# Fixing TensorE's order in a mixture-of-experts stage, and transposing two experts' rows at once

## The chip, the cores and the metric

The kernel runs on one core of a Trainium2 chip. The metric is the device time of one execution in microseconds (us). The core has five engines with queues of their own: TensorE (PE in the profile; PEld is its weight load), VectorE (DVE), ScalarE (ACT), GpSimd (POOL) and SyncE (SP), which here issues most of the DMA transfers.

## The reference

Two layers of a transformer over 512 latent and 256 context tokens of width 1024, float32. Each layer has four mixers (convolution, gating, neighbourhood attention, latent attention) and then a mixture of 32 experts, of which each token takes two. The change touches only the mixture:

```
def hier_moe(h, w_grp, b_grp, w_exp, b_exp, w_gate, w_up, w_down):
    # routing: the best of 4 groups, in it the best 2 of 8 experts, with weights
    ...
    # for every expert e, over the rows routed to it:
    #   y = (silu(rows @ w_gate[e]) * (rows @ w_up[e])) @ w_down[e]      1024 -> 512 -> 1024
    # result of a token: the weighted sum over its two experts
x = x + g2 * f
```

Layer 0 does this for 768 tokens, layer 1 for the 512 latent ones. The weights of one expert are 6 MB (w_gate and w_up 1024 x 512, w_down 512 x 1024, float32), 201 MB a layer.

## The kernel before, in words

Experts are taken in an order with fixed row capacities. In layer 0 they are 96, 96, 32, 32, 128, 32, 128, ..., and the last twelve 64, 96, 64, 96, 64, 64, 96, 64, 96, 96, 64, 64; in layer 1 96, 96, 32, 32, 32, 96, 32, 96, ..., 96, 96, 32, 32, 32, 32. An expert is named here by its place in this order.

**Weights.** SyncE's queue streams them from HBM into 34 slots of 512 KB (tiles named `u`, `xa`, `xb`, `xc`, hi and lo; eight transfers at most are under way). gate and up of an expert are 8 slots, down is 4. `load()` issues as far as slots are free; a slot comes free when TensorE has done its last matmul with it. The weights of experts 0 and 1 and part of 2's are in place before routing is done; those of expert 3 wait for gate_up(0)'s slots, later ones for gate_up(1)'s and down(1)'s.

**Rows.** `gather(g)` fetches the rows of a group of experts from DRAM with an indirect DMA on GpSimd (L1728) into one of three buffers `xb`. A group is one expert, or two neighbours of at most 64 rows each, which then stand at partitions 0 and 64. `rows(e)` (L1381) turns an expert's rows into columns with eight transposes into PSUM (`xTw`), which VectorE copies to `XT` (L1383), one set of eight per expert.

**Products.** `products` (L1414) does the matmuls of `gate_up(e)` and `down(e)`. Rows beyond 64 make a second part: 96 rows are a part of 64 (each matmul with 512 columns of the result) and one of 32 (256 columns). Within a part neighbouring matmuls go to different columns of the array (`tile_position`). ScalarE does the silu (L1429) and VectorE the product (L1430); `hT(e)` (L1449) transposes these inner values for `down(e)`. ScalarE (layer 0, L1472) or VectorE (layer 1, L1474) copies down's result out, and GpSimd scatters it to DRAM (L1775).

**Order.** The loop runs over `seq`: gu0, gu1, d0, gu2, d1, ..., gu31, d30, d31, with hT(e-1) and rows(e+1) written behind gate_up(e). A scheduler builds each engine's list of instructions; it may move transposes and products of independent tiles past each other.

**The tail.** The last two experts of layer 0 (four of layer 1) are not scattered. `tail_table` builds, over the last third of the loop, a matrix that places their rows (`tail_place`, L1350, L1352); `tail_scale` (L1366) spreads the gate weights over a [128, 1024] tile (ScalarE copy L1368), by which `tail_rows` (L1483, VectorE) multiplies the tail experts' results as they come. After the loop, for each of the six (four) tiles of 128 tokens, `accumulate` adds what was scattered and reloaded (`yload`, L1817: ScalarE scales one of the token's two rows, L1492, VectorE does L1495 to L1497), a product `tailw` (L1804) adds the tail (L1805), and `finish` begins the next norm (L1824 to L1831).

## Time and profile before

| | |
|---|---|
| median of 3 runs | 1890.05 us (1889.16 to 1890.92) |
| the profiled execution | 1890.17 us, span 1888.0 us |
| mean granted TensorE clock | 0.961 |
| mixture of layer 0 | from 484.77 us (first xTw) to the last addition that ends at 1048.37 us |
| mixture of layer 1 | from 1366.45 us (first xTw) |

Times in the trace are microseconds from the span's start. A row of the timeline joins neighbouring instructions of one kind (x16: sixteen of them); the releaser in brackets is what ended the idle time before it.

### The profile page before, as it was taken

To read this page: it belongs to the slowest core of one execution; us is meant where nothing else is said; L and a number is where in the kernel's file an instruction comes from. 1 tells how busy PE (TensorE), PEld (TensorE's weight loads), DVE (VectorE), ACT (ScalarE), POOL (GpSimd) and SP (SyncE) were. 2 spreads that over 40 slices of the span, in tenths; PEclk is the share of its full clock that TensorE was granted. 3 is DMA by queue.
4 is the path that set the end of the run, shared out by engine and by line. 5 is a ranking of instruction groups with operands and counts; after the bars stand their busy time and mean duration, and the time that the engine had idled before them with its cause. 6 is when DMAs were issued, how large, how long until landed. Compare 5 with 4: busy or idle time off the path is not lost. (4 is left out here: it accounts for less than half of the span.)

```text
span 1888.0 us, 32569 instructions
## 1 busy us (share of the span) xinstructions
PE 1736.6 (92%) x12876; PEld 1009.1 (53%) x12876; DVE 741.8 (39%) x1611; ACT 471.4 (25%) x862; POOL 222.3 (12%) x255
## 2 busy tenths in 40 slices
PE   6999999997899999999998999999699999988984
PEld 3787788876354433333332788776544334333331
DVE  4566466546310111111115766664623222222235
ACT  4453364322021111111113554732200000000001
POOL 1000100113111110101001001002311101001010
PEclk9999999999799999999999999999799999999997
DMA  8358965453899999999995333428399999999995
GB/s 309 104 188 276 314 228 184 157 221 145 331 404 411 408 401 402 397 415 396 408 373 212 96 90 100 144 72 303 114 387 410 413 412 405 404 404 409 410 413 237
DMA packets 168638, 562.00 MB, mean 298 GB/s; under 512 B 22537, under 2 KB 49225, under 8 KB 139041
## 3 DMA queue, kind: packets, MB, share of 16 engines
q1 hardware_dynamic: 141040, 499.68, 68.9%
q0 software_dynamic: 23264, 54.28, 7.9%
q10 hardware_dynamic: 4176, 5.91, 0.9%
q8 instruction: 104, 1.70, 0.4%
q14 instruction: 54, 0.43, 0.1%
HBM read 543.70 MB, written 38.08 MB: 308 GB/s over the span
## 5 line engine op out<-in xcount | busy, mean ns | idle before, releaser
L1414 PE MATMUL gate_up<-u,XT 128*32 128x256 f32 (+1 forms) x1608 | 277.6, 495 | 10.5 <-DMA u<-in_w_up 8.1
L1429 ACT ACTIVATE eh<-gate_up 64x512 f32<-64x512 f32 (+1 forms) x87 | 43.6, 501 | 763.8 <-PE gate_up L1414 743.2
L1414 PE MATMUL gate_up<-xb,XT 128*32 128x256 f32 (+1 forms) x1160 | 212.2, 484 | 4.1 <-DMA xb<-in_w_up 2.9
L1414 PE MATMUL gate_up<-xa,XT 128*32 128x256 f32 (+1 forms) x816 | 171.4, 476 | 7.5 <-DMA xa<-in_w_up 4.6
L1414 PEld LDWEIGHTS gate_up<-u,XT 128*32 128x32 f32 (+1 forms) x1608 | 94.1, 126 | 140.0 <-issue 99.0
L1430 DVE TENSOR_TENSOR eh<-eh,gate_up 64x512 f32<-64x512 f32 (+1 forms) x87 | 50.5, 580 | 275.7 <-ACT eh L1429 273.9
L193 PE MATMUL zunits<-hT,hi 128*128 128x512 f32 (+1 forms) x384 | 140.2, 366 | 0.9 <-ACT cqs L687 0.8
L194 PE MATMUL zunits<-hT,hi 128*128 128x512 f32 (+1 forms) x384 | 136.2, 355 | 0.0
L195 PE MATMUL zunits<-hT,lo 128*128 128x512 f32 (+1 forms) x384 | 135.4, 353 | 0.0
L1383 DVE COPY XT<-xTw 128x512 f32<-128x512 f32 (+3 forms) x64 | 46.9, 733 | 216.9 <-PE gate_up L1414 209.8
L1414 PEld LDWEIGHTS gate_up<-xb,XT 128*32 128x32 f32 (+1 forms) x1160 | 70.9, 124 | 103.6 <-issue 80.3
L1414 PE MATMUL down<-u,ehT 128*32 128x256 f32 (+1 forms) x736 | 117.0, 478 | 0.9 <-DMA u<-in_w_down 0.6
L1775 POOL DMA_INDIRECT yd<-ey,dst x58 | 53.4, 920 | 516.0 <-ACT ey L1472 256.6
L1414 PE MATMUL gate_up<-xc,XT 128*64 128x512 f32 (+1 forms) x352 | 109.9, 516 | 2.3 <-DMA xc<-in_w_up 2.3
L1414 PE MATMUL down<-xb,ehT 128*32 128x256 f32 (+1 forms) x584 | 96.1, 504 | 6.5 <-DMA xb<-in_w_down 4.6
L1474 DVE TENSOR_TENSOR ey<-down,bc 32x256 f32<-32x256 f32 (+1 forms) x112 | 57.7, 516 | 95.3 <-PE down L1414 94.1
L1381 PE MATMUL xTw<-cpack,xb 64*128 64x64 f32 (+3 forms) x512 | 75.2, 284 | 21.7 <-DVE XT L1383 10.0
L1381 PEld LDWEIGHTS xTw<-cpack,xb 64*128 64x128 f32 (+3 forms) x512 | 63.2, 200 | 58.7 <-issue 24.8
L1414 PEld LDWEIGHTS gate_up<-xa,XT 128*32 128x32 f32 (+1 forms) x816 | 53.6, 121 | 73.6 <-issue 53.7
L1472 ACT COPY ey<-down 64x512 f32<-64x512 f32 (+1 forms) x114 | 54.0, 473 | 141.8 <-PE down L1414 140.8
L174 DVE TENSOR_TENSOR lo<-u,hi 128x1024 fp32r<-128x1024 f32 (+2 forms) x54 | 65.5, 1217 | 47.9 <-ACT hi L168 47.5
L193 PEld LDWEIGHTS zunits<-hT,hi 128*128 128x128 f32 x384 | 72.8, 190 | 16.0 <-issue 4.2
(394 smaller groups left out, 2853.9 us busy)
## 6 DMA issues: line engine op xcount, KB each, us to landing
u<-in_w_gate SPq DMA_DIRECT2D x114, 512.0 KB
u<-in_w_up SPq DMA_DIRECT2D x108, 512.0 KB
u<-in_w_ada SPq DMA_DIRECT2D x96, 512.0 KB
u<-in_w_down SPq DMA_DIRECT2D x87, 512.0 KB
xb<-in_w_down SPq DMA_DIRECT2D x41, 1024.0 KB
xb<-in_w_gate SPq DMA_DIRECT2D x36, 1024.0 KB
xb<-in_w_up SPq DMA_DIRECT2D x35, 1024.0 KB
xa<-in_w_gate SPq DMA_DIRECT2D x24, 1024.0 KB
```

Source lines behind the costliest of these rows:

```text
L174: self.nc.vector.tensor_sub(o, v, h.bitcast(F32))
L193: mm(out, a[0], b[0], start=start, stop=False)
L194: mm(out, a[0], b[1], start=False, stop=False)
L195: self.lastm = mm(out, a[1], b[0], start=False, stop=stop)
L1381: nc.tensor.transpose(ps[:, k * 128:k * 128 + W], Xv[:, :, k], self.ident[a:a + W, a:a + W])
L1383: nc.vector.tensor_copy(xt, ps.rearrange("p (k n) -> p k n", k=8)[:, :, 0:W])
L1414: self.lastm = self.nc.tensor.matmul(o, x[:, k, a:a + w], m[k // q][:, k % q, c], start=(k == 0), stop=(k == K - 1), tile_position=(0, b))
L1429: self.lasta = nc.scalar.activation(v, ps[0:r, 0:c], AF.Silu)
L1430: self.lastv = nc.vector.tensor_mul(v, v, ps[64:64 + r, 0:c])
L1472: self.nc.scalar.copy(y[a:a + w, c], p[0:w, :])
L1474: self.nc.vector.tensor_mul(y[a:a + w, c], p[0:w, :], g2[b:b + w, c])
L1775: nc.gpsimd.indirect_dma_start(out=self.yd[l][:, :], in_=y, in_offset=None, out_offset=bass.IndirectOffsetOnAxis(ap=R["dst"][0:cap[e], ord ...
```

## The change

All of TensorE's work in the mixture now goes through a helper `chain`, which ties each instruction behind the one before it in the program's order; the scheduler no longer mixes them. The program's order itself changes: ahead of gate_up(e) stand hT(e-1) and rows(e+1) (for e = 0 rows(1), for e = 1 rows(2); hT(0) comes behind gate_up(1)). `rows` transposes both experts of a group at once: 49 sets of eight in place of 64 over the two layers. The tail's table pauses ahead of its matmuls in place of behind them. In layer 0 the two additions that were made behind gate_up(31) are made after the loop.

```diff
@@ -1324,7 +1324,7 @@
             nc.vector.tensor_scalar_mul(rhs[:, 32 * i:32 * i + 32], id32, c)
         yield
         ps = self.pss("tail_table")
-        nc.tensor.matmul(ps[:, 0:64], self.ones[0:32, :], rhs, start=True, stop=True)
+        self.chain(nc.tensor.matmul, ps[:, 0:64], self.ones[0:32, :], rhs, start=True, stop=True)
         yield
         nc.vector.tensor_copy(SL, ps[:, 0:64])
         posf = pp.tile([128, NB], F32, name=f"tpos{l}")
@@ -1345,15 +1345,16 @@
             nc.vector.tensor_tensor(eq.rearrange("p (k i e) -> p k i e", k=2, i=NTL),
                                     self.spread[:, 0:TR].unsqueeze(1).unsqueeze(1).to_broadcast(sh),
                                     ta[:, 2 * t:2 * t + 2, :].unsqueeze(3).to_broadcast(sh), op=OP.is_equal)
+            yield
             ps = self.pss("tail_place")
             for k in range(2):
-                nc.tensor.matmul(ps[:, 0:128], eq[:, 128 * k:128 * k + 128], self.ident, start=(k == 0), stop=(k == 1))
+                self.chain(nc.tensor.matmul, ps[:, 0:128], eq[:, 128 * k:128 * k + 128], self.ident, start=(k == 0),
+                           stop=(k == 1))
             for k in range(2):
-                nc.tensor.matmul(ps[0:1, 128:256], R["gate"][:, t, k:k + 1], eq[:, 128 * k:128 * k + 128], start=(k == 0),
-                                 stop=(k == 1))
+                self.chain(nc.tensor.matmul, ps[0:1, 128:256], R["gate"][:, t, k:k + 1], eq[:, 128 * k:128 * k + 128],
+                           start=(k == 0), stop=(k == 1))
             nc.scalar.activation(self.G[:, t * 128:t * 128 + 128], ps[:, 0:128], AF.Copy)
             nc.vector.tensor_add(gr[:, 128 * m:128 * m + 128], gr[:, 128 * m:128 * m + 128], ps[0:1, 128:256])
-            yield
         self.gr = gr
 
     def tail_scale(self, g2):
@@ -1363,22 +1364,27 @@
         for h in range(2):
             c = slice(h * 512, (h + 1) * 512)
             for m, g in enumerate(g2):
-                self.nc.tensor.matmul(ps[:, c], self.gr[:, 128 * m:128 * m + 128], g[0:1, c], start=(m == 0),
-                                      stop=(m == len(g2) - 1))
+                self.chain(self.nc.tensor.matmul, ps[:, c], self.gr[:, 128 * m:128 * m + 128], g[0:1, c], start=(m == 0),
+                           stop=(m == len(g2) - 1))
         self.nc.scalar.activation(o, ps, AF.Copy)
         return o
 
 
+    def chain(self, op, *a, **k):
+
+        with nullcontext() if self.lastm is None else self.tc.issue_after(self.lastm.ins):
+            self.lastm = op(*a, **k)
+
     def xt_tile(self, mp):
         return mp.tile([128, D], F32, tag="XT", name=self.nm("XT"), bufs=2)
 
-    def rows(self, mp, X, a, W):
+    def rows(self, mp, X, W):
 
         nc = self.nc
         ps = self.psw("xTw")
-        Xv = X[a:a + W, :].rearrange("p (d k) -> p d k", k=8)
+        Xv = X[0:W, :].rearrange("p (d k) -> p d k", k=8)
         for k in range(8):
-            nc.tensor.transpose(ps[:, k * 128:k * 128 + W], Xv[:, :, k], self.ident[a:a + W, a:a + W])
+            self.chain(nc.tensor.transpose, ps[:, k * 128:k * 128 + W], Xv[:, :, k], self.ident[0:W, 0:W])
         xt = self.xt_tile(mp)[:, 0:8 * W].rearrange("p (k t) -> p k t", k=8)
         nc.vector.tensor_copy(xt, ps.rearrange("p (k n) -> p k n", k=8)[:, :, 0:W])
         return xt
@@ -1411,8 +1417,8 @@
             for k in range(K):
                 for o, b, m, c in st:
                     q = m[0].shape[1]
-                    self.lastm = self.nc.tensor.matmul(o, x[:, k, a:a + w], m[k // q][:, k % q, c], start=(k == 0),
-                                                       stop=(k == K - 1), tile_position=(0, b))
+                    self.chain(self.nc.tensor.matmul, o, x[:, k, a:a + w], m[k // q][:, k % q, c], start=(k == 0),
+                               stop=(k == K - 1), tile_position=(0, b))
             out.append((ps, [y[0] for y in st]))
         return out
 
@@ -1446,7 +1452,8 @@
             r, n = hv.shape[0:2]
             p = pt[0:n, 256 * i:256 * i + 4 * r]
             for k in range(4):
-                nc.tensor.transpose(p[:, k * r:(k + 1) * r], hv[:, :, k], self.ident[64 * i:64 * i + r, 64 * i:64 * i + r])
+                self.chain(nc.tensor.transpose, p[:, k * r:(k + 1) * r], hv[:, :, k],
+                           self.ident[64 * i:64 * i + r, 64 * i:64 * i + r])
             if n == 128:
                 nc.vector.tensor_copy(o[:, :, a:a + w], p.rearrange("p (k t) -> p k t", k=4))
             else:
@@ -1730,11 +1737,14 @@
                                          bounds_check=NA // 2 - 1, oob_is_err=False)
 
         def rows(e):
-            if e < NE:
-                g, a = place[e]
-                xt[e] = self.rows(mp, X[g], a, parts[e][-1][0] + parts[e][-1][1])
-                if e == groups[g][-1]:
-                    gather(g + 3)
+
+            if e < NE and e == groups[place[e][0]][0]:
+                g = place[e][0]
+                z = groups[g][-1]
+                x = self.rows(mp, X[g], place[z][1] + parts[z][-1][0] + parts[z][-1][1])
+                for i in groups[g]:
+                    xt[i] = x[:, :, place[i][1]:]
+                gather(g + 3)
 
         gather(0)
         self.overflow(l, R, src, pp, mp, XB[1:])
@@ -1746,6 +1756,7 @@
             g2 = [self.bc(self.bc_tile(pp), l, 3, 0)]
             fg = self.bc_tile(pp)
             nc.gpsimd.dma_start(fg, A["final_norm_g"].to_broadcast([128, D]))
+        self.lastm = None
         rows(0)
         load()
         tt = self.tail_table(l, pp, mp, R, T)
@@ -1756,14 +1767,17 @@
             for x in held.pop(("y", t)):
                 x[1] = False
 
-        na = {("gu", NE - 1): 2, ("d", NE - 2): 2} if l == 0 else {("gu", NE - 2): 1, ("d", NE - 3): 3}
+        na = {("d", NE - 2): 2} if l == 0 else {("gu", NE - 2): 1, ("d", NE - 3): 3}
         for i, (m, e) in enumerate(seq):
             if m == "gu":
+
+                if e > 1:
+                    ht[e - 1] = self.hT(mp, h.pop(e - 1), parts[e - 1])
+                rows(e + 1)
                 h[e] = self.gate_up(mp, xt.pop(e), parts[e], *raw.pop((m, e)))
                 done_with(i)
-                if e > 0:
-                    ht[e - 1] = self.hT(mp, h.pop(e - 1), parts[e - 1])
-                rows(e + 1)
+                if e == 1:
+                    ht[0] = self.hT(mp, h.pop(0), parts[0])
             else:
                 if e == NE - 1:
                     ht[e] = self.hT(mp, h.pop(e), parts[e])
```

Three places show what moves. Names: `xTw` are transposed rows, `gate_up`, `down`, `hT` results and inner values in PSUM; `u`, `xa`, `xb`, `xc` with a number are slots of weights, except `xb_0` to `xb_2` in an `xTw` row, which are the gathered rows.

TensorE, the start of layer 0's mixture, before: expert 0's rows, gate_up(0) with its 64 and its 32 rows, then the rows of experts 1 and 2.

```order
L1519 COMPARE_AND_BRANCH
L1519 UNCONDITIONAL_BRANCH
L1381 MATMUL xTw_5512<-cpack,xb_0_5101 128x96 x8
L1414 MATMUL gate_up_5543<-u_5087,XT_5521 64x512
...
L1414 MATMUL gate_up_5560<-xa_0_5077,XT_5521 32x256 x2
L1381 MATMUL xTw_5597<-cpack,xb_1_5102 128x96 x8
L1381 MATMUL xTw_5696<-cpack,xb_2_5103 128x32 x8
L1414 MATMUL gate_up_5629<-xa_1_5078,XT_5606 64x512
```

The same place after the change:

```order
L1526 COMPARE_AND_BRANCH
L1526 UNCONDITIONAL_BRANCH
L1376 MATMUL xTw_5512<-cpack,xb_0_5101 128x96 x8
L1376 MATMUL xTw_5542<-cpack,xb_1_5102 128x96 x8
L1376 MATMUL gate_up_5557<-u_5087,XT_5521 64x512
...
L1376 MATMUL gate_up_5574<-xa_0_5077,XT_5521 32x256 x2
L1376 MATMUL xTw_5628<-cpack,xb_2_5103 128x96 x8
L1376 MATMUL gate_up_5643<-xa_1_5078,XT_5551 64x512
```

The rows of expert 1 have moved ahead of gate_up(0), and one set (of experts 2 and 3 together) stands between the two gate_ups in place of two.

TensorE, late in layer 0, before: down(27) (`down_8405`) with the tail's scaling between its halves, then gate_up(29) (`gate_up_8421` and `gate_up_8438`, its 64 and its 32 rows) with the transposes of expert 28's inner values in it.

```order
L1414 MATMUL down_8405<-xa_0_5077,ehT_8368 64x512 x4
L1366 MATMUL tail_scalew_8687<-xb_4_5086,gr_7484 128x512 x2
L1414 MATMUL down_8405<-xa_1_5078,ehT_8368 64x512 x4
L1366 MATMUL tail_scalew_8687<-xb_4_5086,gr_7484 128x512 x2
L1414 MATMUL gate_up_8421<-xa_2_5079,XT_8383 64x512
L1414 MATMUL gate_up_8438<-xa_2_5079,XT_8383 32x256 x2
L1449 MATMUL hT_8475<-cpack,eh_8312 128x64 x4
L1449 MATMUL hT_8475<-cpack,eh_8312 64x64 x4
L1414 MATMUL gate_up_8421<-xb_0_5082,XT_8383 64x512
```

The same place after the change (down(27) is `down_8339`, gate_up(29) `gate_up_8379` and `gate_up_8396`), and further on down(30) (`down_8593`) with what follows it:

```order
L1376 MATMUL down_8339<-xa_0_5077,ehT_8247 64x512 x4
L1376 MATMUL down_8339<-xa_1_5078,ehT_8247 64x512 x4
L1376 MATMUL hT_8354<-cpack,eh_8264 128x64 x4
L1376 MATMUL hT_8354<-cpack,eh_8264 64x64 x4
L1376 MATMUL xTw_8367<-cpack,xb_0_5101 128x128 x8
L1376 MATMUL gate_up_8379<-xa_2_5079,XT_8262 64x512
...
L1376 MATMUL down_8593<-xb_0_5082,ehT_8567 64x512 x4
L1376 MATMUL down_8593<-xb_1_5083,ehT_8567 64x512 x4
L1376 MATMUL tail_scalew_8602<-xb_4_5086,gr_7429 128x512 x4
L1376 MATMUL hT_8618<-cpack,eh_8573 128x64 x4
```

The transposes stand in front of gate_up(29), those of the rows of experts 30 and 31 in one set, and the tail's scaling has moved behind down(30).

ScalarE at the end of layer 0's mixture, before: silu of expert 30 (`eh_8553`), the copy of the tail's scaling (L1368), down(29)'s result, silu of expert 31, then the scalings of reloaded rows (L1492).

```order
L1429 ACTIVATE eh_8553<-gate_up_8554 64x512
L1368 ACTIVATE u_5089<-tail_scalew_8687 128x1024
L1472 COPY ey_8623<-down_8597 64x512 x2
L1472 COPY ey_8623<-down_8606 32x256 x4
L1429 ACTIVATE eh_8643<-gate_up_8644 64x512
L1492 ACTIVATE xc_1_5081<-xc_1_5081,gate_5158 128x1024
L1492 ACTIVATE xc_0_5080<-xc_0_5080,gate_5158 128x1024
L1492 ACTIVATE u_5093<-u_5093,gate_5158 128x1024
L1796 ACT_TABLE_LOAD
```

The same place after the change; the first row is the silu of expert 31, the copy is L1369.

```order
L1435 ACTIVATE eh_8573<-gate_up_8574 64x512
L1499 ACTIVATE xc_1_5081<-xc_1_5081,gate_5158 128x1024
L1499 ACTIVATE xc_0_5080<-xc_0_5080,gate_5158 128x1024
L1810 ACT_TABLE_LOAD
L1810 ACTIVATE dum_5273<-gate_5158 1x1
L1499 ACTIVATE u_5093<-u_5093,gate_5158 128x1024
L1499 ACTIVATE u_5095<-u_5095,gate_5158 128x1024
L155 DMA u_8727<-in_w_in 128x4x256
L155 DMA u_8729<-in_w_in 128x4x256
L1369 ACTIVATE u_5089<-tail_scalew_8602 128x1024
L1499 ACTIVATE u_5097<-u_5097,gate_5158 128x1024
```

The copy has moved from before down(29)'s result to behind four scalings of reloaded rows. On VectorE the product with it (`u_5088<-down_8593,u_5089`, twice, L1490) now stands ahead of the first addition (L1502); before, the first addition (L1495) stood ahead of it.

## Rows read from the trace of the kernel before

**Rows 1.** the page, its engine table: busy time (share of span) and instructions

```profile
PE 1736.6 (92%) x12876; PEld 1009.1 (53%) x12876; DVE 741.8 (39%) x1611; ACT 471.4 (25%) x862; POOL 222.3 (12%) x255
```

**Rows 2.** windows: span, PE, PEld, DVE, ACT, POOL busy, PEclk, DMA share, GB/s

```profile
511.00:514.00 3.00, 3.00 (x48) 1.92 (x40) 0.29 (x1) 0.38 (x1) 0.00 (x0) 1.00 0.84 280
520.00:960.00 440.00, 428.85 (x2732) 172.87 (x2725) 66.83 (x129) 68.17 (x143) 45.40 (x48) 1.00 1.01 405
531.00:534.00 3.00, 3.00 (x64) 1.81 (x56) 0.00 (x0) 1.49 (x5) 0.48 (x1) 1.00 0.95 332
962.90:969.70 6.80, 6.28 (x24) 2.42 (x21) 0.99 (x3) 0.00 (x0) 0.00 (x0) 0.50 1.03 414
1392.00:1395.00 3.00, 3.00 (x50) 1.83 (x40) 0.13 (x1) 0.38 (x1) 0.00 (x0) 1.00 0.70 227
1412.00:1415.00 3.00, 3.00 (x54) 1.72 (x56) 2.18 (x4) 0.00 (x0) 0.00 (x0) 1.00 0.88 320
1430.00:1858.00 428.00, 384.73 (x2794) 155.20 (x2790) 121.00 (x244) 18.77 (x39) 39.25 (x44) 0.94 1.01 409
```

**Rows 3.** what SyncE's queue waits for, 1430 to 1858: us in total, times, longest

```profile
SPq L146 <- PE gate_up L1414: 3.9, 14, 0.4
```

**Rows 4.** timeline of SyncE's queue: start, us, line, transfers (gu20's and d29's last)

```profile
790.54 1.61 SPq L146 DMA_DIRECT2D u<-in_w_up  x2
...
955.91 5.51 SPq L146 DMA_DIRECT2D u<-in_w_down  x4
```

**Rows 5.** timeline of TensorE: gate_up(20)'s last piece, down(29)

```profile
799.29 7.08 PE L1414 MATMUL gate_up<-u,XT 128*64 128x512 f32 x30
...
994.55 6.33 PE L1414 MATMUL down<-u,ehT 128*64 128x512 f32 x48
```

**Rows 6.** timeline of TensorE, head of layer 0

```profile
487.37 6.29 PE L1414 MATMUL gate_up<-u,XT 128*64 128x512 f32 x17 [1.05 <-DVE XT L1383]
```

**Rows 7.** timeline of TensorE, head of layer 1

```profile
1366.45 1.54 PE L1381 MATMUL xTw<-cpack,xb 96*128 96x96 f32 x8 [5.25 <-issue]
1369.05 12.38 PE L1414 MATMUL gate_up<-xb,XT 128*64 128x512 f32 x96 [1.05 <-DVE XT L1383]
1381.36 2.12 PE L1381 MATMUL xTw<-cpack,xb 96*128 96x96 f32 x16
```

**Rows 8.** timeline of GpSimd, layer 0, the gather of expert 1's rows

```profile
485.24 1.02 POOL L1728 DMA_INDIRECT xb<-h2d,tok  x1 [4.41 <-SPq L1676]
```

**Rows 9.** transfers issued 484.8 to 486 us: that gather, us to landing

```profile
xb<-h2d,tok POOLq DMA_INDIRECT x1, 7.5
```

**Rows 10.** timeline of GpSimd, layer 1, the gather of expert 1's rows

```profile
1366.85 1.02 POOL L1728 DMA_INDIRECT xb<-h2d,tok  x1 [4.74 <-DVE gi L1727]
```

**Rows 11.** transfers issued 1366.5 to 1367.5 us: that gather, us to landing

```profile
xb<-h2d,tok POOLq DMA_INDIRECT x1, 7.7
```

**Rows 12.** chain that ended last, head of layer 1: start, us, what

```profile
1361.04 4.12 DMA xb<-h2d,tok
...
1383.54 10.68 PE gate_up L1414 x96
```

**Rows 13.** timeline of TensorE, layer 0: gate_up(28) and the tail's scaling

```profile
939.68 1.63 PE L1414 MATMUL gate_up<-u,XT 128*64 128x512 f32 x6
...
941.95 12.08 PE L1414 MATMUL gate_up<-u,XT 128*64 128x512 f32 x90
...
955.82 1.98 PE L1366 MATMUL tail_scalew<-xb,gr 1*128 1x512 f32 x4
```

**Rows 14.** chain that ended last, end of layer 0: VectorE's first and last addition

```profile
1013.72 1.30 DVE xc L1495
...
1047.15 1.22 DVE xres L1805
```

**Rows 15.** timeline of ScalarE, end of layer 0: tail's scaling, fourth scaling

```profile
999.37 1.02 ACT L1368 ACTIVATE u<-tail_scalew 128x1024 f32<-128x1024 f32 x1 [3.99 <-PE down L1414]
...
1020.34 1.15 ACT L1492 ACTIVATE u<-u,gate 128x1024 f32<-128x1024 f32 x1 [0.36 <-DMA u<-yd]
```

## The prediction, made before the changed kernel ran

> **What bounds the kernel now.** I read the page's engine table first, then the windows of the two expert stages, then what SyncE's queue waits for, and last the timelines at the head and the end of each stage. TensorE is busy for 92% of the span [rows 1], so a change of its order looks like the place for a gain. The windows say otherwise: from 520 to 960 us (layer 0) and from 1430 to 1858 us (layer 1) the DMA engines are busy at a share of 1.01 and move 405 and 409 GB/s [rows 2]. That is the weight stream, and it has no gap there. TensorE's waiting in that time is not its own: in layer 1's window SyncE, which issues the weights, waits 3.9 us for gate_up in all, out of 428 us, and the next longest wait for TensorE is shorter [rows 3]. So in the middle of both layers the time is bytes over bandwidth, and TensorE's order, its transposes and its gaps lie beside the stream. The order can matter only where the stream stands still for TensorE: at the heads, where the weights of expert 3 and later need slots that experts 0 and 1 hold, and at layer 0's end, where TensorE has fallen behind the stream.
>
> At the heads the reader is to see short dips: 280 GB/s over 511 to 514 us and 332 over 531 to 534, 227 over 1392 to 1395 and 320 over 1412 to 1415 [rows 2]. Against 405 and 409 GB/s that is 3 x (1 - 280/405) = 0.9 us and 0.5 us lost in layer 0, 1.3 and 0.7 us in layer 1. The first dip of each pair ends as gate_up of expert 1 ends, the second as down of expert 1 ends: the stream already waits for TensorE there, with no slack left.
>
> At layer 0's end TensorE lags. gate_up of expert 20 ends at 806.4 us, 14.2 us after the issue of its last weights was done at 792.2 (790.54 + 1.61) [rows 4, 5]. down of expert 29 ends at 1000.9, 39.5 us after the last issue for it, 961.4 (955.91 + 5.51) [rows 4, 5]. The 25 us between these lags are TensorE's own.
>
> **Term A, the heads (a loss).** Before, TensorE transposes expert 0's rows and goes into gate_up(0) at 487.37 and 1369.05 us; the transposes of experts 1 and 2 stand behind it, 16 in a row for 2.12 us [rows 6, 7]. The changed program puts rows(1) ahead of gate_up(0), and TensorE takes them in that order. rows(1) needs the second gather. It is issued at 485.24 in layer 0 [rows 8] and takes 7.5 us to land [rows 9]; in layer 1 at 1366.85 [rows 10] and 7.7 us [rows 11]. That gives 492.7 and 1374.55 us. Eight transposes of 96 rows take 1.54 us at half clock [rows 7], so gate_up(0) starts near 494.3 and 1376.1: 6.9 and 7.0 us later. Only one set of eight then stands between gate_up(0) and gate_up(1) instead of two, which gives 1.06 us back (2.12 / 2): gate_up(1) ends 5.9 us later. The queued transfers cover some of that, but the stream already stood idle for gate_up(1) in both layers, so its next loads move with it. At the second dip the stream is late enough no longer to wait for down(1), which returns 0.5 and 0.7 us. I take 5.9 - 0.5 = **+5.4 us** in layer 0 and 5.9 - 0.7 = **+5.2 us** in layer 1. Bounds: +2.0 if the second gather takes the 4.12 us of the first one in layer 1, the nearest other row [rows 12], and +7 if the longer idle time also keeps the clock at half for 1.5 us more of gate_up(0).
>
> A rule of the Trainium skill stands against the 7.5 us. "DMA: Bandwidth & Descriptors", section "Anatomy of one DMA — SWDGE (gpsimd) path", gives about 2.0 us plus bytes over 436 GB/s. For 96 rows of 4 KB (0.39 MB) an estimate from that page is 2.9 us; gate_up(0) would start 2.3 us later and the heads would cost about 0.7 us each, with a time near 1878. The two rows, measured beside a weight stream that the change leaves as it is, say more than twice that, and I go by them.
>
> **Term B, layer 0's end (a gain).** In the trace gate_up of a 96-row expert late in layer 0 is cut into pieces: 1.63 us of it at 939.68, then transposes of two kinds in turn, then 12.08 us to 953.95, 14.3 us in all [rows 13]. The same 96 matmuls in one piece take 10.68 us in layer 1 [rows 12]. The change keeps every gate_up in one piece. From 806.4 to 1000.9 there are five of them (experts 21, 23, 26, 28, 29): 5 x 3.6 = 18 us. The tail's scaling, four matmuls in 1.98 us and the same again [rows 13], moves from down(27) to behind down(30): 4 us. From 962.9 to 969.7 the granted clock is 0.50, right after these matmuls of one row [rows 2]: half of 6.8, 3.4 us. Two pairs save a set of 1.06 us each: 2 us. The 194.5 us shrink to about 167, and with the stream's own delay of 5.4 us TensorE could end down(29) at 806.4 + 5.4 + 167 = 979. Now the stream sets a floor too: last issue 961.4 + 5.4 + the lag of 14.2 seen where TensorE keeps up = 981. I take **980**, 21 us before 1000.9, with a range of 975 to 987.
>
> What follows keeps only part. Behind down(29) come the last scatter of results, the reload of them, and VectorE's first addition at 1013.72, 12.8 us after down(29); VectorE's chain then runs to its last addition at 1047.15 + 1.22 with few waits [rows 14]. In the changed program ScalarE's copy of the tail's scaling stands behind four scalings of reloaded rows and a table load, and VectorE's product with it (twice) stands ahead of the first addition. The fourth scaling started at 1020.34 and took 1.15 us [rows 15]: 20.6 us after down(29). A copy of 1.02 us [rows 15] and two products of 0.6 us (an estimate: half of VectorE's 1.22 us for 1024 columns) make 22.8. The reloads will also run beside the last weights, which land until about 992; I allow 2 us. So VectorE's chain starts 25 us after down(29) instead of 12.8, at 1005 instead of 1013.7: **-8.7 us**. Bounds: 975 and 22.8 give -16, 987 and 26 give -0.7. If d29 ended after 988.7 nothing would be gained.
>
> **Term C.** Pairing takes away 15 sets of eight transposes (64 become 49), some 16 us of TensorE and 15 copies on VectorE. Two of them are in term B. The rest lie beside a stream at a share of 1.01 [rows 2], so 0; without that cover they would be worth 1.06 us each. The new waits in TensorE's order, hT(e-1) and rows(e+1) ahead of gate_up(e), are covered by down(e-2); a transposition of inner values needs ScalarE and VectorE behind gate_up(e-1), 1.02 + 1.22 us at the most by the larger operations of [rows 14, 15], and down(e-2) is work of about that length or longer. Layer 0's accumulations that move from expert 31's gate_up to after the loop are in the 25 us.
>
> **Sum.** -8.7 (with layer 0's head in it) + 5.2 (layer 1, which stays stream-bound to its end and keeps what its head loses) = -3.5 us against the profiled execution's 1890.17, which is 0.12 us over the median of 1890.05: **1886.7 us**.
>
> **Rivals.** (1) *The heads cost little.* If the second gather lands 4.1 us after issue [rows 12], gate_up(0) starts 3.6 us later and gate_up(1) ends 2.5 us later, about +2 in each layer; down(29) ends at 976.6, the chain starts at 1001.6, -12.1 + 2 = -10: 1880. For it: the same instruction took 4.12 us with no weights beside it. Against: both second gathers did run beside weights. (2) *Slower: the scaling's copy on ScalarE takes the whole gain.* VectorE stands still for it behind all four reloads. If down(29) ends at 988.7 or later, or the reloads lose 8.7 us more to the last weights, the chain starts no earlier than before, and layer 1's head remains: 1890.2 + 5.2 = 1895.4. For it: 12.2 of the 21 us are already lost by the count above; against: TensorE's 27 us have rows for each part. (3) *The order hides.* TensorE's pieces turn out no longer at the end than before and the heads' delay is covered by queued transfers: 1890.
>
> **How the numbers follow.** Forecast 1886.7 with its own spread of 1882.5 to 1891: 0.45. Rival 1: 0.20. Rival 2: 0.20. Rival 3: 0.15. 0.2% is 3.8 us, about what a measurement of this kernel can tell, so "faster" is under 1886.3 and "slower" over 1893.8. The forecast lies near that edge: 0.22 of its 0.45 is faster and 0.23 the same. Rival 1 is faster (0.20); of rival 2 0.17 is slower and 0.03 the same, of rival 3 0.13 the same and 0.02 slower. Sum: faster 0.42, same 0.39, slower 0.19. The range 1879 to 1896 leaves out the ends of rivals 1 and 2.
>
> **What would show it.** Right: gate_up(0) starting near 494 and 1376 us behind a wait for the gather; dips in GB/s that are some 5 us wider at each head; gate_up of 96 rows at 10.7 us everywhere; down(29) near 980; VectorE's first addition near 1005, released by the copy on ScalarE; 49 sets of transposes. Wrong: gate_up(0) starting by 491, an unbroken stream at 500 to 515 us, down(29) after 988, or layer 1's stream taking other than 428 us for what it moves between 1430 and 1858.

## The result: slower by half a per cent, and the profile after

The changed kernel took 1898.41 us (median of 5 runs, 1894.71 to 1903.39) against 1889.68 us: the ratio is 1.0051, with a 95% interval of 1.003 to 1.0072. Forecast was 1886.7 us, with a range that ended at 1896. The profiled execution took 1894.71 us (span 1892.9), the fastest of the five.

Most of what the prediction said it would see is in the trace. TensorE's timeline at the two heads, with the wait ahead of a row in brackets:

```profile
493.20 1.54 PE L1376 MATMUL xTw<-cpack,xb 96*128 96x96 f32 x8 [6.00 <-DMA xb<-h2d,tok]
494.68 6.41 PE L1376 MATMUL gate_up<-u,XT 128*64 128x512 f32 x17
...
1370.79 1.54 PE L1376 MATMUL xTw<-cpack,xb 96*128 96x96 f32 x8 [6.78 <-DMA xb<-h2d,tok]
1372.27 12.83 PE L1376 MATMUL gate_up<-xb,XT 128*64 128x512 f32 x96
1385.03 1.13 PE L1376 MATMUL xTw<-cpack,xb 96*128 96x96 f32 x8
```

TensorE stands still for the second gather at both heads, with expert 0's weights and columns ready. gate_up(0) starts at 494.68 (forecast 494.3) in place of 487.37 [rows 6]. In layer 1 it starts 15.2 us after the first gather was issued (1357.04, below); before, that was 8.0 us (1369.05 less 1361.04) [rows 7, 12].

The windows of the weight stream (last two columns: DMA share, GB/s) answer to [rows 2]:

```profile
500.00:505.00 5.00, 5.00 (x40) 1.75 (x40) 0.23 (x1) 0.59 (x1) 0.00 (x0) 1.00 0.59 230
505.00:510.00 5.00, 5.00 (x66) 2.79 (x60) 1.84 (x3) 0.38 (x1) 0.98 (x1) 1.00 0.72 230
...
1378.00:1383.00 5.00, 5.00 (x50) 1.85 (x50) 0.69 (x1) 0.59 (x1) 0.00 (x0) 1.00 0.17 69
1383.00:1388.00 5.00, 5.00 (x58) 2.75 (x52) 1.38 (x2) 0.38 (x1) 0.99 (x1) 1.00 0.71 242
...
1433.00:1843.00 410.00, 357.68 (x2670) 154.64 (x2673) 107.67 (x223) 18.43 (x38) 43.14 (x47) 0.96 1.01 409
```

The dips are wide now: 69 GB/s over 5 us of layer 1 is 4.2 us lost in that one window. The middle of layer 1 runs at 409 GB/s as before, with TensorE busy for 87% of it (357.68 of 410) in place of 90% (384.73 of 428).

The end of layer 0, in TensorE's timeline (gate_up of expert 28, in one piece; down of expert 29) and then in the chain that ended last:

```profile
935.57 10.68 PE L1376 MATMUL gate_up<-u,XT 128*64 128x512 f32 x96
...
977.02 5.47 PE L1376 MATMUL down<-u,ehT 128*64 128x512 f32 x48
```

```profile
984.31 0.91 DMA yd<-ey,dst
985.22 7.32 issue
992.58 0.52 POOL xc L1831
...
994.72 12.98 DMA u<-yd
...
1008.88 1.03 ACT u L1369
...
1010.64 0.69 DVE u L1490
1011.33 1.20 DVE xc L1502
...
1044.03 1.22 DVE xres L1819
...
1357.04 4.20 DMA xb<-h2d,tok
```

down(29) ends at 982.5 (forecast 980, before 1000.9 [rows 5]). But VectorE's first addition (L1502) comes at 1011.3, only 2.4 us earlier than before [rows 14], and directly ahead of it in the chain stand ScalarE's copy of the tail's scaling (L1369) and VectorE's product with it (L1490). Ahead of that stand the reloads (`u<-yd`), 13 us in flight. ScalarE's timeline has the first and the fourth scaling of reloaded rows, which answers to [rows 15]:

```profile
1001.38 1.15 ACT L1499 ACTIVATE xc<-xc,gate 128x1024 f32<-128x1024 f32 x1 [9.10 <-DMA xc<-yd]
...
1007.73 1.15 ACT L1499 ACTIVATE u<-u,gate 128x1024 f32<-128x1024 f32 x1 [0.15 <-DMA u<-yd]
```

A wait that the prediction had taken for covered, in layer 1, on VectorE and on TensorE:

```profile
1402.00 1.39 DVE L1481 TENSOR_TENSOR ey<-down,bc 64x512 f32<-64x512 f32 x2 [3.02 <-PE down L1376]
1403.88 1.73 DVE L1481 TENSOR_TENSOR ey<-down,bc 32x256 f32<-32x256 f32 x4 [0.50 <-PE down L1376]
1405.64 0.42 DVE L1458 COPY ehT<-hT 128x256 f32<-128x256 f32 x1
```

```profile
1403.75 0.69 PE L1376 MATMUL hT<-cpack,eh 64*128 64x64 f32 x4
1406.12 0.46 PE L1376 MATMUL hT<-cpack,eh 64*64 64x64 f32 x4 [1.68 <-DVE ehT L1458]
1406.51 0.41 PE L1376 MATMUL gate_up<-xc,XT 128*32 128x256 f32 x2
```

hT(1) has two parts, of 64 and 32 rows, in one PSUM tile. The second waits until VectorE has copied the first, and VectorE first does the four pieces of down(0)'s last results (1.73 us). gate_up(2) stands behind it, and starts 2.8 us after hT(1) did. Over layer 1 TensorE waits for that copy ten times, for 15.2 us:

```profile
PE hT L1376 <- DVE ehT L1458: 15.2, 10, 1.7
...
PE xTw L1376 <- DMA xb<-h2d,tok: 6.8, 1, 6.8
```

The kernel before has this wait too, but less of it; for hT(0) and hT(1) the scheduler put transposes of rows between the two parts:

```profile
PE hT L1449 <- DVE ehT L1451: 8.5, 7, 1.8
```

Right behind hT(1)'s wait TensorE's granted clock fell from 1.00 to 0.50 (1.2 GHz) for 3.4 us, in both traces of the changed kernel, and gate_up(2) took 5.3 us, where it takes 3.7 in the kernel before. Such a wait did not always bring the clock down: the run "head and scaling" has the same waits and stayed at 1.00 there. One window of it (last columns: clock, DMA share, GB/s):

```profile
1407.50:1410.50 3.00, 3.00 (x36) 1.54 (x32) 0.00 (x0) 0.00 (x0) 0.00 (x0) 0.50 1.03 400
```

To compare traces, I cut each span at three events, since executions differ by some us ahead of the first: the issue of layer 0's first gather, VectorE's first addition behind layer 0's loop, the issue of layer 1's first gather, and the end. The third column is a part of the fourth: up to the issue of layer 1's last weights. Each number is a difference of two times of one trace, in us; the names are those of the runs below.

| trace | layer 0: gather to addition | to layer 1's gather | layer 1: gather to last weights | layer 1: gather to end | median |
|---|---|---|---|---|---|
| before | 533.9 | 347.3 | 498.8 | 527.0 | 1889.7 |
| changed | 530.5 | 345.8 | 506.9 | 535.9 | 1898.4 |
| changed, again | 531.0 | 348.5 | 507.5 | 535.8 | 1898.6 |
| rows(1) late | 525.6 | 348.0 | 501.9 | 531.2 | 1885.5 |
| scaling early | 521.9 | 349.2 | 507.5 | 537.3 | 1889.9 |
| written order | 526.3 | 347.4 | 498.8 | 531.4 | 1886.5 |
| two PSUM tiles | 531.1 | 349.7 | 506.4 | 534.6 | 1895.6 |
| no pairs | 532.5 | 348.0 | 509.6 | 538.8 | 1901.2 |
| head and scaling | 518.6 | 348.9 | 500.6 | 530.5 | 1879.4 |
| three | 517.0 | 349.7 | 498.8 | 527.8 | 1876.4 |
| before, rows(1) ahead | 535.8 | 349.0 | 505.5 | 535.2 | 1902.6 |
| three, additions early | 518.3 | 346.3 | 498.5 | 527.5 | 1873.0 |

The changed kernel gains some 3 us in layer 0's mixture and loses 8.8 us in layer 1's, 8.1 to 8.8 of them by the issue of the last weights. That issue is one row of SyncE's timeline; here it is from four traces: before, changed, "before, rows(1) ahead" and "three", whose first gathers in layer 1 were issued at 1361.04, 1357.04, 1367.02 and 1345.04 us.

```profile
1859.79 0.33 SPq L146 DMA_DIRECT2D u<-in_w_down  x1
1863.94 0.33 SPq L146 DMA_DIRECT2D u<-in_w_down  x1
1872.48 0.33 SPq L146 DMA_DIRECT2D u<-in_w_down  x1
1843.84 0.33 SPq L146 DMA_DIRECT2D u<-in_w_down  x1
```

There is one trace of each kernel, and the table's noise can be read from it: "changed", "changed, again" and "scaling early" have the same program in layer 1 and lie up to 1.5 us apart from gather to end; the two traces of the changed kernel lie 2.7 us apart in the stretch to layer 1's gather.

### The profile page after: what moved, and what is told of

Same layout as the page of the kernel before. It is cut to its first block, busy times and chain, and to the rows that moved or that the text cites. A ratio compares the mean times of both kernels' runs of the same rounds, so it can differ in the third digit from the quotient of the medians.

```text
span 1892.9 us, 32248 instructions
## 1 busy us (share of the span) xinstructions
PE 1686.4 (89%) x12756; PEld 1003.7 (53%) x12756; DVE 740.6 (39%) x1596; ACT 472.2 (25%) x862; POOL 223.7 (12%) x255
## 5 line engine op out<-in xcount | busy, mean ns | idle before, releaser
L1376 PE MATMUL gate_up<-u,XT 128*32 128x256 f32 (+1 forms) x1608 | 260.9, 496 | 12.8 <-DMA u<-in_w_up 12.1
L1436 DVE TENSOR_TENSOR eh<-eh,gate_up 64x512 f32<-64x512 f32 (+1 forms) x87 | 50.4, 580 | 522.0 <-ACT eh L1435 521.9
L1376 PE MATMUL gate_up<-xa,XT 128*32 128x256 f32 (+1 forms) x816 | 166.2, 478 | 9.5 <-DMA xa<-in_w_up 9.5
L193 PE MATMUL zunits<-hT,hi 128*128 128x512 f32 (+1 forms) x384 | 140.5, 366 | 0.9 <-ACT cqs L687 0.8
L1376 PE MATMUL down<-u,ehT 128*32 128x256 f32 (+1 forms) x736 | 103.4, 475 | 4.7 <-DMA u<-in_w_down 3.7
L1376 PE MATMUL down<-xb,ehT 128*32 128x256 f32 (+1 forms) x584 | 90.1, 506 | 12.7 <-DMA xb<-in_w_down 12.1
L193 PEld LDWEIGHTS zunits<-hT,hi 128*128 128x128 f32 x384 | 72.8, 190 | 16.0 <-issue 4.4
L168 ACT ACTIVATE hi<-u 128x1024 fp32r<-128x1024 f32 (+2 forms) x56 | 57.3, 1033 | 86.1 <-PE zunits L194 49.8
L194 PEld LDWEIGHTS zunits<-hT,hi 128*128 128x128 f32 x384 | 72.8, 190 | 11.0 <-issue 1.7
L195 PEld LDWEIGHTS zunits<-hT,lo 128*128 128x128 f32 x384 | 72.6, 189 | 10.6 <-issue 0.6
```

Of the source, the lines that this page charges most:

```text
L168: self.nc.scalar.activation(h, v, AF.Copy)
L193: mm(out, a[0], b[0], start=start, stop=False)
L194: mm(out, a[0], b[1], start=False, stop=False)
L195: self.lastm = mm(out, a[1], b[0], start=False, stop=stop)
L1376: self.lastm = op(*a, **k)
L1436: self.lastv = nc.vector.tensor_mul(v, v, ps[64:64 + r, 0:c])
```

## Experiments

The runs were made in three sets, each on one chip with runs of the kernel before (medians 1890.31, 1889.59 and 1892.32 us). My theory after the result: the loss stands at three places, the wait for the second gather at the heads (A), ScalarE's copy behind the reloads (A too), and hT's wait for VectorE (C). The main rival: a fixed order costs the weight stream something everywhere.

**The changed kernel again.** No edit.

> The changed kernel once more, unedited, for a second trace and as the reference of the other runs of this set. Its five times were 1894.7 to 1903.4 us with a median of 1898.4, and the only trace is that of the fastest of them. Theory A (the wait for expert 1's rows at the two heads, and ScalarE's order at layer 0's end, explain the loss): the second trace shows gate_up(0) starting again some 7 us later than before at both heads, whatever the time. Rival R (TensorE's fixed order costs the weight stream something everywhere): a slower execution shows a longer stretch between the heads and the ends, that is layer 1's weights taking more than the 480 us from the end of gate_up(0) to the last issue that the first trace shows. Median expected 1898, 1895 to 1901.

Measured: 1898.6 us, ratio 1.0055 (1.0036 to 1.0075). gate_up(0) starts 14.1 and 15.1 us after the first gathers (13.8 and 15.2 in the first trace). The trace of this slower execution differs from the first by 2.7 us behind the first addition of layer 0, and by 0.6 us or less in the other columns. The middle of layer 1 moves 408 GB/s. Of the rival that the order costs everywhere little is left, but not nothing. Compared transfer by transfer from 124 to 423 us after layer 1's first gather, SyncE's issues slip by another 0.7 us (changed) and 1.6 us (again) against the kernel before, with the DMA engines at a share of 1.01 in all three. In the other eight traces with the fixed order the slip is 0.6 to 3.0 us, in the one other with the scheduler's order 0.3. What makes it was not tried.

**rows(1) behind gate_up(0) again.**

```diff
-                rows(e + 1)
+                if e > 0:
+                    rows(e + 1)
                 h[e] = self.gate_up(mp, xt.pop(e), parts[e], *raw.pop((m, e)))
                 done_with(i)
+                if e == 0:
+                    rows(1)
```

> Only the head is undone: expert 1's rows are transposed behind gate_up(0) again, as before the change; everything else stays changed. Theory A: gate_up(0) starts 7 us earlier at both heads, the stream's dips shrink to those of before; layer 1 keeps its 7 to 8 us to the end, layer 0 part of its 5. Time 8 to 11 us under the changed kernel of the same set: 1887 to 1890 where that is 1898. Rival R (the order costs everywhere): 0 to 3 us under it. Rival that the heads are covered by queued transfers: no difference.

Measured: 1885.48 us (12 runs), ratio 0.9974 (0.9963 to 0.9984), 13 us under the changed kernel: more than expected. By the table, layer 0 gains 5 us and layer 1 4.6; the 3 us left are more than these stretches account for. TensorE's timeline at layer 1's head:

```profile
1360.62 12.54 PE L1376 MATMUL gate_up<-xb,XT 128*64 128x512 f32 x96 [1.05 <-DVE XT L1389]
1373.10 2.02 PE L1376 MATMUL xTw<-cpack,xb 96*128 96x96 f32 x16
```

Two sets stand behind gate_up(0) in 2.02 us, and the second hides behind VectorE's copy of the first. With this one edit undone the rest of the change is faster than the kernel before.

**The tail's scaling early.**

```diff
             load()
+            if l == 0 and (m, e) == ("d", NE - NTL - 1):
+                Gs = self.tail_scale(g2)
...
-                    if j == 0:
+                    if j == 0 and l == 1:
                         Gs = self.tail_scale(g2)
```

> Only the tail's scaling in layer 0 moves: the four matmuls stand behind down(29) in place of behind down(30), so that ScalarE's copy stands ahead of the scalings of the reloaded rows. Theory A: VectorE's first addition follows the first scaled row, about 1.2 us after the first reload landed, in place of 8.7 us later; VectorE's chain ends 7 to 9 us earlier and the time falls by that: 1889 to 1891 where the changed kernel has 1898. Rival: VectorE's chain is bound by the reloads, which run beside the last weights, and ends within 2 us of where it did; time less by 0 to 2 us.

Measured: 1889.89 us (12 runs), ratio 0.9999 (0.9986 to 1.0012), 8.7 us under the changed kernel, as expected. ScalarE's timeline, and VectorE's first addition:

```profile
986.18 1.02 ACT L1369 ACTIVATE u<-tail_scalew 128x1024 f32<-128x1024 f32 x1 [2.12 <-PE tail_scalew L1376]
...
1001.15 1.15 ACT L1499 ACTIVATE xc<-xc,gate 128x1024 f32<-128x1024 f32 x1 [5.03 <-DMA xc<-yd]
```

```profile
1002.33 1.29 DVE L1502 SCALAR_TENSOR_TENSOR xc<-xc,gate 128x1024 f32<-128x1024 f32 x1 [1.98 <-ACT xc L1499]
```

The addition now follows the first reloaded row, and the gain is kept: layer 0's last addition ends 556.0 us after the first gather, against 564.4 and 565.8 in the two traces of the changed kernel.

**The written order of before, still fixed.**

```diff
-                if e > 1:
-                    ht[e - 1] = self.hT(mp, h.pop(e - 1), parts[e - 1])
-                rows(e + 1)
                 h[e] = self.gate_up(mp, xt.pop(e), parts[e], *raw.pop((m, e)))
                 done_with(i)
-                if e == 1:
-                    ht[0] = self.hT(mp, h.pop(0), parts[0])
+                if e > 0:
+                    ht[e - 1] = self.hT(mp, h.pop(e - 1), parts[e - 1])
+                rows(e + 1)
```

> TensorE's order stays fixed by the program and the pairs stay, but the program's order is that of the kernel before: gate_up(e), then hT(e-1), then rows(e+1). Heads as before, gate_up still in one piece. Theory A: as the run with only the head undone, within 2 us, since in the middle the stream hides TensorE. Rival R2 (hT ahead of gate_up is what costs, by its wait for VectorE, which has four copies of results to do first in layer 1): 3 us or more under that run.

Measured: 1886.54 us (12 runs), ratio 0.9979 (0.9967 to 0.9992), within 1.1 us of the run with rows(1) late. That is as theory A has it, but not for its reason. With hT behind gate_up the last weights of layer 1 are issued 3.1 us earlier (498.8 us after the first gather, as in the kernel before, against 501.9), so hT's place does cost the stream something, as rival R2 has it. At layer 1's end this order loses the same again: the stretch from the last weight issue to the end is 32.6 us, 29.3 with only the head undone. What lengthens it was not tried.

**Both undoings together,** rows(1) late and the scaling early, with the two edits above.

> Both undoings together: expert 1's rows behind gate_up(0) again, and the tail's scaling behind down(29). Alone they stood 13.1 and 8.7 us under the changed kernel of the last set (1898.6). Theory A (two separate places on the path, one at each end of the stage): the gains add, some 20 us under the changed kernel, 1876 to 1880 us, and 10 to 13 us under the kernel before. Rival (both are the same slack, since an earlier down(29) collides more with the last weights): 1884 to 1886, no better than the head alone.

Measured: 1879.40 us, ratio 0.9948 (0.9932 to 0.9965), 19 us under the changed kernel of the first set. The two gains add to within 3 us: they are two places on the path.

**Two PSUM tiles for the inner values,** alone and on top of both.

```diff
+            if i:
+                pt = self.pss("hT")
             p = pt[0:n, 256 * i:256 * i + 4 * r]
```

> The changed kernel with the two PSUM tiles for inner values alone. Theory C: 1 to 3 us under the changed kernel (1898.6 in the last set), 1896 to 1898; the waits of transposes of inner values for VectorE's copy (15.2 us in ten waits in layer 1) vanish from the trace. Rival: no difference.

> As the run with head and scaling, and the inner values of a 96-row expert go to two PSUM tiles in place of one, so that the second four transposes don't wait for VectorE's copy of the first four. Theory C (this wait, at most 1.7 us at a time and 2.7 us of TensorE's standing at gate_up(2) of layer 1, delays the head of layer 1): 1 to 3 us under the run without it. Rival (the stream hides it, and the second tile makes gate_up wait for results that VectorE has yet to copy): within 1 us, or slower.

Measured: alone 1895.58 us (11 runs), ratio 1.0032 (1.0021 to 1.0043), 3 us under the changed kernel; on top of both 1876.40 us, ratio 0.9936 (0.9919 to 0.9953), 3 us under the run without it. The intervals overlap with those they are compared with, but the runs on top of both were made in one set, and each of the five (1875.06 to 1878.09) lies under each of the five without (1878.83 to 1880.71). The trace shows the mechanism. TensorE in layer 1, three edits undone, and a window of the granted clock just behind:

```profile
1384.85 0.69 PE L1376 MATMUL hT<-cpack,eh 64*128 64x64 f32 x8
1385.47 0.41 PE L1376 MATMUL gate_up<-xc,XT 128*32 128x256 f32 x2
```

```profile
1385.50:1389.00 3.50, 3.50 (x65) 1.95 (x64) 2.08 (x6) 0.00 (x0) 0.97 (x1) 1.00 1.04 421
```

Both parts of hT(1) run in 0.69 us without a wait, gate_up(2) follows at once at full clock, and the row of ten waits is gone from TensorE's list. In the table layer 1 falls by 2.7 us where the head does not wait, to 527.8, within 0.8 us of the kernel before. Where the head still waits it falls by 1.2 us, no more than the traces of one program differ by.

**No pairs.** One set for each expert, as before the change; order and the rest changed.

```diff
-            if e < NE and e == groups[place[e][0]][0]:
...
+            if e < NE:
+                g, a = place[e]
+                xt[e] = self.rows(mp, X[g], a, parts[e][-1][0] + parts[e][-1][1])
+                if e == groups[g][-1]:
+                    gather(g + 3)
```

> The changed kernel without the pairs: one set of eight transposes for each expert again, 64 sets in place of 49; order and everything else stay changed. The prediction's term C says that pairing is hidden by the stream: within 1.5 us of the changed kernel (1898.6 in the last set). At the heads one more set of 1.1 us stands between gate_up(0) and gate_up(1), which could add 1 us in each layer. Rival (pairing earns its 16 us of TensorE where TensorE is behind): 5 us or more over it.

Measured: 1901.23 us, ratio 1.0075 (1.0055 to 1.0095), 2.6 us over the changed kernel of the other set (3.8 by the ratios), with intervals that overlap. Pairing is worth 0 to 4 us, not the 16 us of TensorE that it takes away. The traces put 1.7 us into layer 0 and 3.0 into layer 1; rows(3) then stands ahead of gate_up(2) as a set of its own, which would fit, but it was not tried apart.

**The head alone, in the kernel before.** gate_up(0)'s matmuls are tied behind rows(1); the scheduler orders the rest.

```diff
+                self.head = e == 0
+                if e == 0:
+                    rows(1)
                 h[e] = self.gate_up(mp, xt.pop(e), parts[e], *raw.pop((m, e)))
...
+                    with self.tc.issue_after(self.lastx.ins) if self.head else nullcontext():
+                        self.lastm = self.nc.tensor.matmul(...)
```

> The kernel before with one part of the change alone: expert 1's rows are transposed ahead of gate_up(0), which is tied behind them; everything else is as before, the scheduler's order, the 64 sets, the tail's scaling. Theory A (the wait for the second gather at the heads is the largest loss): 8 to 13 us over the kernel before, 1898 to 1903, with gate_up(0) starting 7 us later at both heads. Rival (the head costs only in company of the fixed order, since the scheduler fills TensorE's gap): 0 to 3 us over it.

Measured: 1902.60 us (6 runs), ratio 1.0054 (1.0037 to 1.007), 10 us over the kernel before. TensorE's timeline at the heads:

```profile
494.94 1.54 PE L1381 MATMUL xTw<-cpack,xb 96*128 96x96 f32 x8 [6.34 <-DMA xb<-h2d,tok]
...
1380.90 1.54 PE L1381 MATMUL xTw<-cpack,xb 96*128 96x96 f32 x8 [6.86 <-DMA xb<-h2d,tok]
```

This one part costs as much as the whole change does. Layer 1 takes 8.2 us more, 6.7 of them by the issue of the last weights. hT has no part in that: it waits for its copy 7.0 us in seven waits, less than in the kernel before. gate_up(1) ends 5.0 us later after the first gather and down(1) 6.2 us later, since down(1), which takes 5.5 us in the kernel before, takes 7.2 here; the granted clock was 0.50 in it for 3.4 us:

```profile
1420.00:1423.00 3.00, 3.00 (x10) 0.74 (x8) 0.00 (x0) 0.00 (x0) 0.00 (x0) 0.50 1.00 414
```

Layer 0 takes only 1.9 us more: there, TensorE is behind the stream at the end, so a stream that is late by some us costs little.

**Three undone, and the first additions early again.**

```diff
-        na = {("d", NE - 2): 2} if l == 0 else ...
+        na = {("gu", NE - 1): 2, ("d", NE - 2): 2} if l == 0 else ...
```

> The fastest kernel so far (head, scaling and two PSUM tiles for inner values, 1876.4) with the last undone part of the change: the first two additions of layer 0 are written behind gate_up(31) again. On VectorE this puts the first addition ahead of the product with the tail's scaling. Theory A: that product no longer waits for anything late, so its place is worth its own length at most: 1875 to 1877. Rival (the additions' place in the program is what delays VectorE): 3 us or more under 1876.

Measured: 1872.96 us (4 runs), ratio 0.9901 (0.9884 to 0.9918), the fastest kernel of the study. It lies 3.4 us under the run with three edits by the times and 6.6 by the ratios; the two were not run in one set. In their traces the stretch from layer 0's first gather to layer 1's is 864.5 us against 866.8. The first addition comes 1.2 us later after the first gather, not earlier, and the last one ends 0.5 us later. What is gained stands behind it: the next mixer's first matmul (L193) starts 5.8 us after the last addition's end, against 8.4 with three edits. The last addition and that matmul, with three edits and then in this run:

```profile
1027.89 1.22 DVE L1826 TENSOR_TENSOR xres<-xres,tailw 128x1024 f32<-128x1024 f32 x1
...
1037.46 1.28 PE L193 MATMUL zunits<-hT,hi 128*128 128x512 f32 x3
```

```profile
1029.99 1.22 DVE L1826 TENSOR_TENSOR xres<-xres,tailw 128x1024 f32<-128x1024 f32 x1
...
1037.04 1.15 PE L193 MATMUL zunits<-hT,hi 128*128 128x512 f32 x3 [0.55 <-DVE ht L333]
```

In the nine traces whose additions all come after the loop this stretch is 7.0 to 8.4 us, in the kernel before 5.3. But "before, rows(1) ahead", which also has two additions early, has 7.6, so the cause stays open.

## Why the prediction was wrong, by its own steps

**What bounds the kernel** was right in the main. Over the 410 us from 76 us after layer 1's first gather, all twelve traces moved 407 to 409 GB/s, whatever TensorE's order; most of what the change moves lies at heads and ends, and the slip of 0.6 to 3.0 us in between was not foreseen.

**Term A** had the right mechanism: 6.9 and 7.0 us of delay forecast for gate_up(0); measured, counted from the issue of the first gather, 6.2 us in layer 0 (13.8 against 7.6) and 7.2 in layer 1 (15.2 against 8.0). For layer 1 it was mis-sized: 5.2 us forecast; alone, in the kernel before, the early rows cost 8.2, and undoing them gives back 4.6 to 5.4 where hT waits and 6.8 where it does not. The step that failed in it is the return, "At the second dip the stream is late enough no longer to wait for down(1), which returns 0.5 and 0.7 us". In layer 0 it came, in the first trace: SyncE's issues were 5.2 us late behind gate_up(1), 4.3 behind down(1) and 4.1 at expert 29's weights. In layer 1 the delay grew instead: 6.5 us behind gate_up(1), 7.2 behind down(1), 8.1 at the last weights; with the head alone 5.0, 6.3 and 6.7. The gather's price held: TensorE's transposes began 7.1 us after its issue in layer 0 and 7.9 in layer 1. The formula of the Trainium skill, "DMA: Bandwidth & Descriptors", section "Anatomy of one DMA — SWDGE (gpsimd) path", gives an estimate of 2.9 us for it; the measurement is more than twice that, and rival 1, which needed a short gather, did not come.

**Term C** is the other step that failed in layer 1: "The new waits in TensorE's order, hT(e-1) and rows(e+1) ahead of gate_up(e), are covered by down(e-2)". I had counted ScalarE's silu and VectorE's product as what hT needs. hT also needs its PSUM tile back from VectorE between its two parts, and in layer 1 VectorE has down(e-2)'s results to copy at that very moment, the work that I took for cover. Where the head is on time the wait's price is some 3 us: layer 1 takes 530.5 and 531.2 us with it and 527.8 and 527.5 without, and the last weights are issued 1.8 to 3.4 us later with it. Where the head is late too, layer 1 takes 534.6 us without it and 535.8, 535.9 and 537.3 with it. The two delays do not simply add: the head alone makes 8.2 us, the wait some 3, both together 8.8. Why they overlap is not shown. The wait delays gate_up(2) and so down(1), but the way to the end is not by down(1) alone: with two PSUM tiles and the head late, down(1) ended 4.0 to 4.6 us earlier than in the two traces of the changed kernel, and the last weights came only 0.5 to 1.1 us earlier. That pairing itself costs or brings little was right to within 4 us.

**Term B** had the gain of TensorE right and the rest too short. down(29) was to end 21 us earlier; counted from the first gather it ended 19.5 us earlier (501.6 against 521.1). VectorE's additions were to start 25 us behind it and started 28.8 us behind it. The failed number is "I allow 2 us" for reloads beside the last weights: it was 6. From the end of down(29) to ScalarE's fourth scaling it was 19.5 us before (1020.34 less 1000.88 [rows 5, 15]) and 25.2 after (1007.73 less 982.49), 5.8 more: the reload was issued 8.3 us after the scatter (984.31 to 992.58), in place of 4.1, and the first reload came 8.8 us later. So of the 8.7 us forecast some 3 were gained. The run with the scaling early gives 9 us back: the copy's place took most of the gain, as rival 2 put it. Rival 2 asked for down(29) at 988.7 or reloads 8.7 us later to take all of it; neither came in full. That its sum, 1895.4 us, is nearest to what was measured is luck: it is made of 0 at layer 0's end and 5.2 in layer 1, and the traces have a gain of 3 and a loss of 8.8.

**The sum.** Against the forecast, layer 0's end is worse by 5.5 us (3.2 gained by the table, 8.7 forecast) and layer 1 by 3.6: 1886.7 + 9.1 = 1895.8, between the two profiled executions (1894.7 and 1897.2). Up to 2.6 us more lie behind the last addition, which the prediction did not look at: the next mixer's first matmul comes 7.0 and 7.5 us after it in the two traces, 5.3 before. Counted to that matmul layer 0 gained 2.5 and 0.6 us, and the sum is 1896.5 and 1898.4, beside executions of 1894.7 and 1897.2 and a median of 1898.4. One to two us stay open.

## What to carry to other kernels

An order that is fixed by the program also fixes its waits: ahead of each instruction that starts a stage, ask which later operand's load it now stands behind. Here eight transposes moved ahead of a product cost as much as the whole change; without that, and with one copy in an earlier place, the rest of it was worth 10 us.

When a faster engine brings the end of a stage nearer, read what is still in flight there: reloads that found little traffic before (62 GB/s) found the last weights now (382 GB/s), and a copy that nobody waited for came to stand ahead of the first addition.

A wait is covered by other work only if the engine that ends the wait is free meanwhile. Here TensorE's down(e-2) was to cover hT's wait for VectorE, and VectorE had down(e-2)'s results to copy first.

## What the runs showed that I had not expected

A scatter and a reload of unchanged size took about twice as long beside the weight stream. Between the issue of the last scatter and that of the reload lay 4.1 us before, in which the DMA engines moved 62 GB/s, and 8.25 us after, at 382 GB/s. The first reloads, of 1 MB, landed 6.0 us after their issue before and 10.7 us after. Windows of either trace, and those reloads' issues (the kernel before, then the changed one):

```profile
1003.36:1007.46 4.10, 4.10 (x22) 1.43 (x20) 0.00 (x0) 0.00 (x0) 0.91 (x1) 1.00 0.22 62
...
xc<-yd POOLq DMA_DIRECT2D x2, 1024.0 KB, 6.0
```

```profile
984.31:992.56 8.25, 7.79 (x34) 2.44 (x32) 0.25 (x1) 0.59 (x1) 0.91 (x2) 1.00 0.92 382
...
xc<-yd POOLq DMA_DIRECT2D x2, 1024.0 KB, 10.7
```

The trace names gate_up as the releaser of GpSimd's wait there, but with the scaling early gate_up(31) ended at 995.5 us and the reload was issued at 992.3 all the same. That the scatter waits its turn behind queued weights fits these rows; it was not measured by itself.
